# Five of twelve mixer gate pairs as seven block products, in a decoder block on one core

## The chip, the cores and the metric

The kernel runs on one core of a Trainium2 chip. The core has five engines with an instruction stream each: TensorE (PE in the profile, its weight loads PEld), VectorE (DVE), ScalarE (ACT), GpSimd (POOL) and SyncE (SP), which here only starts transfers. Transfers by the core's 16 DMA engines are started from a queue of SP, ACT or POOL. The metric is the device time of one execution in microseconds (us), lower is better; the time before is the median of three runs, 1539.44 us (1537.3 to 1540.5).

## The reference

One decoder block, fp32, 256 tokens, D = 2048. Cut to what matters:

```python
proj = rmsnorm(x, mix_norm_w) @ w_in        # q, k, v, g, gk_low, gate_b, gate_c, xc, merge_a, merge_b
o    = rmsnorm(gla_chunked(q, k, v, log_g), gla_norm_w)          # 4 heads of 512 values
y_a  = o * silu(g)
y_b  = gate_b * causal_depthwise_conv(gate_c * xc, conv_w)       # 3 taps over tokens
merged = sigmoid(merge_a) * y_a + sigmoid(merge_b) * y_b
h    = x + merged @ w_out
gate, up = split(rmsnorm(h, ffn_norm_w) @ w_gate_up)             # 2 x 5632 columns
h    = h + (silu(gate) * up) @ w_down
out  = rmsnorm(h, final_norm_w)
```

The six gates g, gate_b, gate_c, xc, merge_a and merge_b have 2048 columns each. They are the names g, gb, gc, xc, ma and mb below, each cut into four groups of 512 columns (gc0 to gc3 and so on), and fg, fu are the halves of w_gate_up.

## The kernel before

**Precision and tiling.** Every fp32 operand is held as two parts, hi (rounded, made by a cast on ScalarE, L200) and lo (the remainder, a subtraction on VectorE, L205). A product takes three matmuls (lo by hi, hi by lo, hi by hi, L309 to L311 in `mm3`). The two token halves of 128 (t = 0, 1) are the stationary side, and 512 weight columns move, so a group of 512 columns costs 16 row chunks x 2 token halves x 3 = 96 matmuls of 128x512. Weights come in pieces of 128x1024 (512 KB, two row chunks of 512 columns), one DMA each on SP's queue. `stream_list` fixes the order of all pieces, and `load_piece` works five pieces ahead of the one in use: fetch, cast, subtraction. So VectorE's stream is a chain of L205 rows with everything else between them, and it serves TensorE in the order of the pieces. A sum of weights is a piece too: it has its own cast and its own subtraction.

**Stages.** Up to about 206 us: k, q, v of the four heads with the gated linear attention; to 733 us: the 24 gate groups in the order gc, xc, gb, g, ma, mb for each of the four column groups i, all with eight block products; to 824 us: wo (w_out, four groups); then the feed-forward part (FFN) in three parts, each with its hidden groups and then its rows of w_down (dn). Helper work is put into the stream by `later(n, ...)`, `at(n, ...)` and `one_at_a_time(n, ...)`, which run a function when a count of used pieces (the tick) has gone on by n; a scheduler then places each instruction on its engine.

**Block products.** Seen as a product of 2x2 blocks (two token halves by two row chunks on one side, two row chunks by two column groups on the other), a pair of groups needs eight block products, or seven if sums of blocks are multiplied. The FFN before does five of its eleven pairs fg/fu (`SEVEN`, L73) with seven, in `sevens`: 28 pieces of 6 matmuls, 168, where two groups take 192. For each quarter q of the rows the pieces are 11, t1, t3, t2 and t4, and after all quarters 21 and 22; t1 to t4 are sums of weight blocks made by VectorE (L221, L227), and some weight pieces are read twice. The sums of the activations' blocks (hsum, L431 and following) are made when h is transposed. Such a pair is mixed piece by piece with a pair done with eight (`merged`).

**Attention and gates.** In a head, the scores go to PSUM (sc_ps), VectorE masks them (L619) and splits them into sch (ScalarE) and scl (VectorE, L624), and TensorE multiplies them with v (o_ps, `attend`). TensorE takes its instructions in order, so what stands behind an o_ps matmul waits with it. The convolution multiplies u = gc xc and two copies of u shifted by one and two tokens with the taps; the copies are DMAs inside the core's memory, issued on ScalarE's queue (L681 to L686), and VectorE reads them at L692 and L691. A group of merged columns is transposed on TensorE (trb, L440) before wo.

Of the kernel before, what the change touches and what calls it, by code (L numbers as in the profile page):

```python
# [72 lines left out]
SEVEN = (0, 2, 4, 6, 9)  # L73
# [12 lines left out]
def seven_list(f):  # L86

    out = [(what, q) for q in range(4) for what in ("11", "t1", "t3", "t2", "t4")]
    return [(f"s{f}", e) for e in out + [(what, q) for q in range(4) for what in ("21", "22")]]


def eight_list(f):
    return [(f"{m}{f}", k) for m in ("fg", "fu") for k in range(0, KC, 2)]


SPREAD = (("t1", "t3", "t2", "t4"), ("21", "22"))


def merged(part):

    f0, f1 = PARTS[part]
    sevens = [e for f in range(f0, f1) if f in SEVEN for e in seven_list(f)]
    eights = [e for f in range(f0, f1) if f not in SEVEN for e in eight_list(f)]

    gaps = [0] * len(sevens)
    rest = len(eights)
    while rest > 0:
        for some in SPREAD:  # L110
            for n, e in enumerate(sevens):
                if e[1][0] in some and rest > 0:
                    gaps[n] += 1
                    rest -= 1
# [4 lines left out]
    return out + eights[put:]  # L119


def down_list(part):

    f0, f1 = PARTS[part]
    ends = {}
    for i, (key, _) in enumerate(merged(part)):
        ends[int(key.lstrip("sfgu"))] = i
# [10 lines left out]
def stream_list():  # L138

    pieces = [(p[0], p[3]) for p in piece_list()]  # L140
    out = [e for e in pieces if e[0][:2] not in ("fg", "fu", "dn")]
    for part in range(len(PARTS)):
        out += merged(part)
        out += down_list(part)
# [4 lines left out]
def block_kernel(ctx, tc, x, xt, cols_in, gkw_in, gku_in, gnw, conv_w, finw, w_in, w_out, w_gu, w_dn, out):  # L149
# [4 lines left out]
    res = ctx.enter_context(tc.tile_pool(name="res", bufs=1))  # L154
# [4 lines left out]
    aT = ctx.enter_context(tc.tile_pool(name="aT", bufs=1))  # L159
    psum = ctx.enter_context(tc.tile_pool(name="psum", bufs=1, space=bass.MemoryType.PSUM))  # L160
# [46 lines left out]
    def sum_of(key, what, q):  # L207

        fg, fu = key.replace("s", "fg"), key.replace("s", "fu")
        if what == "21":  # L210
            return fetch(fg, 4 * q + 2)
        if what == "22":
            return fetch(fu, 4 * q + 2)
        if what == "11":
            held["y"] = fetch(fg, 4 * q, dpool, "y")
            return held["y"]
        y = held["y"]
        if what == "t1":
            held["x"] = fetch(fu, 4 * q, dpool, "x")
# [3 lines left out]
        if halfway and halfway[-1][0] is held["x"]:  # L223
            finish_low()
        other = y if what == "t2" else fetch(fu if what == "t3" else fg, 4 * q + 2)
        x = held["x"]
# [86 lines left out]
    def tok_piece(ps, t, piece, k0, first, last, ah, al):  # L313
# [684 lines left out]
```

## Time and profile before

| what | value |
|---|---|
| runs before, median (lowest to highest) | 1539.44 us (1537.3 to 1540.5) |
| profiled execution: its own time, its span | 1539.7 us, 1537.7 us |
| clock granted to TensorE in it | 0.998 |
| busy: TensorE, VectorE, ScalarE | 99%, 68%, 50% of the span |
| matmuls (profiled), pieces of weights | 7249, 612 |

A row of a timeline reads: start in us, duration in us, engine, line of the kernel, operation, output<-inputs, shape, xcount, and in brackets how long the engine sat idle before it and what released it. Successive rows of VectorE overlap by some hundredths of a us, so the time from start to start is the price of a row in a full stream. The table of windows gives for each stretch its length, then the busy time of PE, PEld, DVE, ACT and POOL with their counts, the granted clock, the share of the DMA engines and GB/s.

### The profile page before, as it was taken

The numbers are of one execution on the slowest core, as the hardware profiler recorded it, in microseconds if no ns is written. First come the engines' busy times: TensorE is split into PE (matmuls) and PEld (weight loads), VectorE is DVE, ScalarE is ACT, GpSimd is POOL, SyncE is SP. The second block draws the span as 40 slices with busy tenths as digits, with TensorE's granted clock in tenths as the row PEclk, the third lists the DMA queues.
The fourth block names the chain that finished last, engine by engine and source line by source line (L and its number), as shares of the span: only waits on it lengthen the run. The fifth ranks groups of instructions, "written<-read, shape, count | busy, mean of one in ns | idle before, by whom it ended". The sixth has DMA issues, their size and how long they took to land.

```text
span 1537.7 us, 19268 instructions
## 1 busy us (share of the span) xinstructions
PE 1526.0 (99%) x7249; PEld 1279.2 (83%) x7249; DVE 1040.8 (68%) x1047; ACT 771.8 (50%) x870; POOL 17.7 (1%) x29
## 2 busy tenths in 40 slices
PE   9999999999999999999999999999999999999998
PEld 8989988888888888888888888788888888888887
DVE  6765545655655655465668999855899985678764
ACT  6763454444344344444556565643555653455543
POOL 0020000000000000000000000000000000000000
PEclk9999999999999999999999999999999999999999
DMA  9655566766866666666755877866677886566772
GB/s 321 220 165 177 175 197 190 244 194 192 239 193 191 211 221 190 203 208 194 230 174 176 259 225 236 302 212 181 219 247 222 266 273 195 180 221 202 248 222 92
DMA packets 91846, 327.11 MB, mean 213 GB/s; under 512 B 10381, under 2 KB 10509, under 8 KB 91625
## 3 DMA queue, kind: packets, MB, share of 16 engines
q1 hardware_dynamic: 88320, 316.99, 65.3%
q10 hardware_dynamic: 3432, 8.89, 2.4%
q8 instruction: 57, 0.93, 0.3%
q14 instruction: 37, 0.30, 0.1%
HBM read 319.57 MB, written 2.10 MB: 209 GB/s over the span
## 4 chain that ended last, share of the span: by engine, by line
PE 92%; DVE 4%; issue 1%; DMA 1%; ACT 1%; POOL 1%; DVEq 0%; SPq 0%; ACTq 0%
PE dn L309 5%; PE dn L311 5%; PE dn L310 5%; PE p L309 3%; PE p L311 3%; PE p L310 3%; PE fu L309 3%; PE fu L310 3%; PE fu L311 3%; PE fg L310 2%; PE fg L311 2%; PE fg L309 2%; PE wo L310 2%; PE gc L311 2%; PE mb L310 2%; PE ma L310 2%
## 5 line engine op out<-in xcount | busy, mean ns | idle before, releaser
L205 DVE TENSOR_TENSOR lo<-raw,hi 128x1024 fp32r<-128x1024 f32 (+1 forms) x533 | 648.6, 1221 | 369.0 <-PE dn L309 73.0
L200 ACT CAST hi<-raw 128x1024 fp32r<-128x1024 f32 (+1 forms) x533 | 556.8, 1051 | 566.8 <-PE dn L311 113.9
L309 PE MATMUL dn<-lo,acth 128*128 128x512 f32 (+1 forms) x376 | 141.9, 377 | 0.2 <-DVE sg L810 0.2
L310 PE MATMUL dn<-hi,actl 128*128 128x512 f32 (+1 forms) x376 | 141.2, 376 | 0.0
L311 PE MATMUL dn<-hi,acth 128*128 128x512 f32 (+1 forms) x376 | 141.1, 376 | 0.0
L200 ACT CAST hi<-x 128x1024 fp32r<-128x1024 f32 x60 | 63.2, 1054 | 104.0 <-DVE x L227 68.0
L205 DVE TENSOR_TENSOR lo<-x,hi 128x1024 fp32r<-128x1024 f32 x60 | 73.4, 1223 | 19.9 <-ACT hi L200 12.5
L309 PEld LDWEIGHTS dn<-lo,acth 128*128 128x128 f32 x376 | 70.8, 188 | 13.6 <-DVE sg L810 0.6
L311 PEld LDWEIGHTS dn<-hi,acth 128*128 128x128 f32 x376 | 70.8, 188 | 12.8
L310 PEld LDWEIGHTS dn<-hi,actl 128*128 128x128 f32 x376 | 70.8, 188 | 12.7
L309 PE MATMUL fu<-lo,hh 128*128 128x512 f32 x192 | 74.9, 390 | 0.2 <-DVE sg L810 0.2
L311 PE MATMUL fg<-hi,hh 128*128 128x512 f32 x192 | 74.9, 390 | 0.0
L309 PE MATMUL fg<-lo,hh 128*128 128x512 f32 x192 | 74.8, 390 | 0.0
L310 PE MATMUL fg<-hi,hl 128*128 128x512 f32 x192 | 74.8, 390 | 0.0
L310 PE MATMUL fu<-hi,hl 128*128 128x512 f32 x192 | 74.7, 389 | 0.0
L311 PE MATMUL fu<-hi,hh 128*128 128x512 f32 x192 | 74.7, 389 | 0.0
L309 PE MATMUL p<-lo,sh 128*128 128x512 f32 x160 | 62.9, 393 | 0.0
L311 PE MATMUL p<-hi,sh 128*128 128x512 f32 x160 | 62.4, 390 | 0.0
L310 PE MATMUL p<-hi,sl 128*128 128x512 f32 x160 | 62.3, 390 | 0.0
L227 DVE TENSOR_TENSOR x<-x,raw 128x1024 f32<-128x1024 f32 x40 | 48.8, 1220 | 2.5 <-DMA raw<-in_w_gu_dram 2.3
L309 PE MATMUL v<-lo,xh 128*128 128x512 f32 x128 | 50.4, 394 | 0.0
L309 PE MATMUL wo<-lo,mh 128*128 128x512 f32 x128 | 50.2, 392 | 0.0
(236 smaller groups left out, 3152.5 us busy)
## 6 DMA issues: line engine op xcount, KB each, us to landing
raw<-in_w_in_dram SPq DMA_DIRECT2D x255, 512.0 KB, 4.3
raw<-in_w_gu_dram SPq DMA_DIRECT2D x176, 512.0 KB, 4.6
raw<-in_w_dn_dram SPq DMA_DIRECT2D x88, 512.0 KB, 4.4
raw<-in_w_out_dram SPq DMA_DIRECT2D x32, 512.0 KB, 3.6
y<-in_w_gu_dram SPq DMA_DIRECT2D x20, 512.0 KB, 3.7
x<-in_w_gu_dram SPq DMA_DIRECT2D x20, 512.0 KB, 5.5
u<-u ACTq DMA_DIRECT2D x8, 448.0 KB, 7.2
taps<-in_conv_w_dram ACTq DMA_DIRECT2D x4, 768.0 KB
```

The costliest lines, as they stand in the source:

```text
L200: nc.scalar.copy(hi[:, ks, :], raw[:, ks, :])
L205: nc.vector.tensor_tensor(out=lo[:, ks, :], in0=raw[:, ks, :], in1=hi[:, ks, :].bitcast(F32), op=ALU.subtract)
L227: nc.vector.tensor_tensor(out=x, in0=x, in1=other, op=ALU.add)
L309: nc.tensor.matmul(ps, lhsT=sh, rhs=ml, start=first, stop=False, skip_group_check=onto)
L310: nc.tensor.matmul(ps, lhsT=sl, rhs=mh, start=False, stop=False, skip_group_check=onto)
L311: nc.tensor.matmul(ps, lhsT=sh, rhs=mh, start=False, stop=last, skip_group_check=onto)
```

## The change

**Gates.** Five pairs, (gc0,xc0), (gc1,xc1), (gc2,xc2), (gc3,xc3) and (gb3,mb3), are done as seven block products. `GATES` gives six steps; in each the 28 pieces of the pair are mixed with the pieces of the eight-product groups beside it, in step 4 with a gap after the 11 pieces too. Steps 1 to 5 hold 2, 3, 4, 2 and 2 eight-product groups. The sums of blocks of x that the pairs need (`x_blocks`, four quarters of L714, four L438 and one L440 on VectorE, one cast on ScalarE) are made during attention. `HIDDEN` writes down the same mix for the FFN as before. The pieces grow from 612 to 672, the matmuls fall by 120.

**Element-wise work.** SiLU comes from ScalarE in one activation instead of a sigmoid and a multiplication on VectorE, for g and in the FFN. The head outputs o are normed in `head_norm` during attention, one head at a time, instead of in the gates. gb0 to gb2 leave PSUM by ScalarE. The sigmoids of ma0 to ma3 and mb0 to mb2 go to one buffer, scr, from which VectorE multiplies (L848). The convolution is cut into `conv_shift` (the copies) and `conv_sum` (VectorE's five rows L827 to L831). ScalarE now changes between SiLU and sigmoid in the gates: it has 17 table loads instead of 10.

**Buffers and transfers.** h is no tile of its own during the mixer any more. x is read for its squares into two buffers taken in turn (xq), and again, late, into h: four transfers of 512 KB from GpSimd's queue behind wo's first group.

```diff
-SEVEN = (0, 2, 4, 6, 9)
+GATES = (
+    (None, ("g0",)),
+    (("gc0", "xc0"), ("ma0", "gb0")),
+    (("gc1", "xc1"), ("mb0", "g1", "ma1")),
+    (("gc2", "xc2"), ("gb1", "mb1", "g2", "ma2")),
+    (("gc3", "xc3"), ("gb2", "mb2")),
+    (("gb3", "mb3"), ("g3", "ma3")),
+)
...
+HIDDEN = (
+    ((("fg0", "fu0"), ("fg1", "fu1")), (("fg2", "fu2"), ("fg3", "fu3"))),
+    ((("fg4", "fu4"), ("fg5", "fu5")), (("fg6", "fu6"), ("fg7", "fu7"))),
+    ((("fg9", "fu9"), ("fg8", "fu8", "fg10", "fu10")),),
+)
...
+def mixed(step, early=False):
+
+    pair, keys = step
...
+        for some in (sums + ("11",) if early else sums, ("21", "22")):
+            for n, (_, e) in enumerate(sevens):
...
+def gates_list():
+    return [e for i, step in enumerate(GATES) for e in mixed(step, i == 4)]
...
+    def eights(key, a, done, tags=("b5", "ax1")):
...
+    def sevens(name, pool, a, s, second, done):
...
+            elif what == "t2":
+                quad(pc, lambda j: s(1, q, j), piece, first, last)
+                if last:
+                    u[1] = second(1)
+                    nc.vector.tensor_tensor(out=v2, in0=pc, in1=v2, op=ALU.subtract)
+                    nc.vector.tensor_tensor(out=v3, in0=pd, in1=v2, op=ALU.add)
+                    nc.vector.tensor_tensor(out=u[1], in0=pb, in1=v3, op=ALU.add)
+            elif what == "t4":
+                quad(pe, lambda j: a(1, 4 * q + 2 + j), piece, first, last)
+                if last:
+                    nc.vector.tensor_tensor(out=v3, in0=pe, in1=v3, op=ALU.subtract)
+                    done(1, v3, u[1])
...
+    def sum_blocks(raw, q, tiles, work):
+
+        hi, lo = tiles
+        a11, a21 = raw[:, 0:2, 0:P], raw[:, 0:2, P:T]
+        a12, a22 = raw[:, 2:4, 0:P], raw[:, 2:4, P:T]
+        for s, p, m in ((0, a21, a22), (1, a11, work[:, 0]), (2, a21, a11), (3, a12, work[:, 1])):
+            nc.vector.tensor_tensor(out=work[:, s], in0=p, in1=m, op=ALU.subtract)
+        nc.scalar.copy(hi[:, q], work)
+        nc.vector.tensor_tensor(out=lo[:, q], in0=work, in1=hi[:, q].bitcast(F32), op=ALU.subtract)
...
+    xq = {}
+
+    def load_x(j):
+        xq[j] = gpool.tile([P, NT, 512], F32, tag=("exk", "exq")[j % 2], name="xq")
+        nc.sync.dma_start(xq[j], xv[:, :, j * 512:(j + 1) * 512])
...
+    def x_blocks(q):
+        pair = gpool.tile([P, NM, T], F32, tag="bc", name="xraw")
+        raw, work = pair[:, 0:4, :], pair[:, 4:8, :].rearrange("p s (j c) -> p s j c", c=P)
+        cs = slice(4 * q, 4 * q + 4)
+        nc.vector.tensor_tensor(out=raw, in0=xh[:, cs, :].bitcast(F32), in1=xl[:, cs, :].bitcast(F32), op=ALU.add)
+        sum_blocks(raw, q, xsums, work)
+
+    for q in range(4):
+        at(34 + 6 * q, lambda q=q: x_blocks(q))
...
+    def head_norm(i):
+        rstd_of(sso[:, :, i], DV, ro[:, :, i])
+        for t in range(NT):
+            nc.vector.scalar_tensor_tensor(out=o[i][:, t, :], in0=o[i][:, t, :], scalar=ro[:, t, i:i + 1], in1=gnb,
+                                           op0=ALU.mult, op1=ALU.mult)
...
+    def gated(dst, ps):
+
+        for t in range(NT):
+            scr = ew.tile([P, 512], F32, tag="scr", name="scr")
+            nc.scalar.activation(scr, ps[t], AF.Sigmoid, scale=r1[:, t:t + 1])
+            nc.vector.tensor_tensor(out=dst[:, t, :], in0=dst[:, t, :], in1=scr, op=ALU.mult)
...
+    def gate(key):
+        i = int(key[-1])
+
+        def done(ps):
+            if key[:-1] == "g":
+                ya[i] = ew.tile([P, NT, 512], F32, tag="ya", name="ya")
+                for t in range(NT):
+                    nc.scalar.activation(ya[i][:, t, :], ps[t], AF.Silu, scale=r1[:, t:t + 1])
+                nc.vector.tensor_tensor(out=ya[i], in0=ya[i], in1=o[i], op=ALU.mult)
+            elif key[:-1] == "gb":
+                sb[i] = ew.tile([P, NT, 512], F32, tag="sb", name="sb")
+                for t in range(NT):
+                    nc.scalar.activation(sb[i][:, t, :], ps[t], AF.Copy, scale=r1[:, t:t + 1])
+            elif key[:-1] == "ma":
+                gated(ya[i], ps)
+            else:
+                gated(sb[i], ps)
+                merge(i, slice(0, NT))
...
+            if pair[0][:-1] == "gc":
+                nc.vector.scalar_tensor_tensor(out=two, in0=one, scalar=r1sq[:, t:t + 1], in1=two,
+                                               op0=ALU.mult, op1=ALU.mult)
+                if t == 0:
+                    later(2, lambda: conv_shift(i))
+                    later(8, lambda: conv_sum(i))
+            else:
+                nc.scalar.activation(two, two, AF.Sigmoid, scale=r1[:, t:t + 1])
+                nc.vector.scalar_tensor_tensor(out=two, in0=one, scalar=r1[:, t:t + 1], in1=two,
+                                               op0=ALU.mult, op1=ALU.mult)
+
+                later(3 if t else 1, lambda: merge(i, slice(t, t + 1)))
...
+    steps = run(gates_list(), begin_gate)
+    for n in steps:
...
+        if h is None:
+            mix.close()
+            dpool = ctx.enter_context(tc.tile_pool(name="dpool", bufs=1))
+            h = dpool.tile([P, NT, D], F32, name="h")
+            for j in range(4):
+                nc.gpsimd.dma_start(h[:, :, j * 512:(j + 1) * 512], xv[:, :, j * 512:(j + 1) * 512])
...
-        nc.scalar.activation(dst, src, AF.Sigmoid, scale=r2[:, t:t + 1])
-        times(dst, src, t)
+        nc.scalar.activation(dst, src, AF.Silu, scale=r2[:, t:t + 1])
```

VectorE in attention, where the scores of heads 0 and 1 are masked and split (L741 and L746 after are L619 and L624 before). Before:

```order
L603 TENSOR_TENSOR exk<-exk,kr 128x256
L205 TENSOR_TENSOR lo<-raw,hi 128x1024 x3
L619 COPY_PREDICATED scr<-mask,sc_ps 128x256
L624 TENSOR_TENSOR scl<-scr,sch 128x384
L205 TENSOR_TENSOR lo<-raw,hi 128x1024
L619 COPY_PREDICATED scr<-mask,sc_ps 128x256
```

And with the change, from the row behind exk on, where L714, L438 and L440 are `x_blocks`:

```order
L714 TENSOR_TENSOR xraw<-xh,xl 128x1024
L222 TENSOR_TENSOR lo<-raw,hi 128x1024
L438 TENSOR_TENSOR xraw<-xraw 128x256 x3
L222 TENSOR_TENSOR lo<-raw,hi 128x1024
L438 TENSOR_TENSOR xraw<-xraw 128x256
L222 TENSOR_TENSOR lo<-raw,hi 128x1024
L440 TENSOR_TENSOR sl<-xraw,sh 128x1024
L741 COPY_PREDICATED scr<-mask,sc_ps 128x256
L714 TENSOR_TENSOR xraw<-xh,xl 128x1024
L746 TENSOR_TENSOR scl<-scr,sch 128x384
L222 TENSOR_TENSOR lo<-raw,hi 128x1024
L438 TENSOR_TENSOR xraw<-xraw 128x256 x2
```

The second mask (L741) is the next row. Six instructions of sums stand ahead of the first mask and three more between it and the second; TensorE's order there is as before.

VectorE where the third convolution begins, before (xc, the third group of its kind) and with the change (start of step 4):

```order
L205 TENSOR_TENSOR lo<-raw,hi 128x1024 x13
L711 SCALAR_TENSOR_TENSOR u<-xc_0_4123,r_117,u 128x512
L205 TENSOR_TENSOR lo<-raw,hi 128x1024
L711 SCALAR_TENSOR_TENSOR u<-xc_1_4124,r_117,u 128x512
L694 TENSOR_TENSOR yb<-u,taps 128x1024
L205 TENSOR_TENSOR lo<-raw,hi 128x1024
L692 TENSOR_TENSOR u_4294<-u_4294,taps 128x1024
```

```order
L411 TENSOR_TENSOR u<-gc_1_3847,v_3851 128x512
L882 SCALAR_TENSOR_TENSOR u<-gc_0_3846,r1sq,u 128x512
L222 TENSOR_TENSOR lo<-x,hi 128x1024
L848 TENSOR_TENSOR ya<-ya,scr 128x512
L244 TENSOR_TENSOR x<-x,y 128x1024
L848 TENSOR_TENSOR ya<-ya,scr 128x512
L828 TENSOR_TENSOR u_4836<-u_4836,taps 128x1024
L222 TENSOR_TENSOR lo<-raw,hi 128x1024
```

Between the last write of u and the first row that reads a copy (L692, now L828) lay two rows of VectorE, and now lie four; the rows around it now belong to a stream with sums of weights in it (L244).

ScalarE at the same place with the change, where L814 to L819 issue the copies:

```order
L847 ACT_TABLE_LOAD
L847 ACTIVATE scr<-ma_0_4595,r_115 128x512
L814 DMA u_4836<-u 112x1024
L847 ACTIVATE scr<-ma_1_4596,r_115 128x512
L815 DMA u_4836<-u 15x1024
```

A table load and the sigmoid of ma2 stand ahead of the first copy; before, the copies stood ahead of or between casts only.

More of the change, by code (lines that the diff above doesn't have):

```diff
@@ L109, in merged @@
     while rest > 0:
-        for some in SPREAD:
-            for n, e in enumerate(sevens):
-                if e[1][0] in some and rest > 0:
+        for some in (sums + ("11",) if early else sums, ("21", "22")):
+            for n, (_, e) in enumerate(sevens):
+                if e[0] in some and rest > 0:
                     gaps[n] += 1
```

424 lines of the change are left out of this document (205 added, 219 removed).

## The prediction

> **What bounds the kernel now.** I read the page first: its head, its first part and the chain of the work that ended last.
>
> ```profile
> span 1537.7 us, 19268 instructions
> PE 1526.0 (99%) x7249; PEld 1279.2 (83%) x7249; DVE 1040.8 (68%) x1047; ACT 771.8 (50%) x870; POOL 17.7 (1%) x29
> PE 92%; DVE 4%; issue 1%; DMA 1%; ACT 1%; POOL 1%; DVEq 0%; SPq 0%; ACTq 0%
> ```
>
> TensorE is busy nearly throughout and is the chain, so a matmul taken away is time, if VectorE (68% on average) can still feed it. That average hides two kinds of stages, which the table of windows parts. Its rows are attention around head 0, the 24 gate groups, and the first two FFN hidden parts:
>
> ```profile
> core 0: us, PE busy (x) PEld busy (x) DVE busy (x) ACT busy (x) POOL busy (x), PEclk, DMA share, GB/s
> 82.00:108.00 26.00, 25.05 (x122) 20.55 (x121) 16.72 (x25) 17.12 (x21) 5.67 (x7) 1.00 0.57 181
> 206.00:733.00 527.00, 527.00 (x2338) 436.75 (x2337) 299.02 (x274) 230.34 (x239) 4.08 (x8) 1.00 0.68 206
> 823.70:992.40 168.70, 168.38 (x758) 138.13 (x756) 157.73 (x155) 103.52 (x116) 0.00 (x0) 1.00 0.77 248
> 1080.60:1247.60 167.00, 166.88 (x749) 137.62 (x748) 154.03 (x147) 96.39 (x102) 0.00 (x0) 1.00 0.76 250
> ```
>
> In the gates VectorE works 299 of 527 us, 57%; in the hidden parts, where half the pairs are done as sevens already, 158 of 168.7, 93%. The groups of VectorE in the gates say what it does in its idle time there:
>
> ```profile
> L205 DVE TENSOR_TENSOR lo<-raw,hi 128x1024 fp32r<-128x1024 f32 x192 | 234.5, 1224 | 192.8 <-PE xc L309 42.7 <-PE mb L309 37.3 <-PE ma L309 35.9
> ```
>
> Its 192.8 us of idling before L205 ended with TensorE: it waits for buffers, so it is ahead. The change spends this spare time to buy matmuls.
>
> **The saving.** One matmul's price is the distance of starts in the gates, here the first and the 57th row of TensorE's timeline:
>
> ```profile
> 379.65 0.39 PE L309 MATMUL xc<-lo,xh 128*128 128x512 f32 x1
> 392.35 0.39 PE L311 MATMUL gb<-hi,xh 128*128 128x512 f32 x1
> ```
>
> 12.70 us / 56 = 0.2268 us. A pair falls from 192 to 168 matmuls; five pairs save 120 x 0.2268 = 27.2 us. All else is what VectorE loses of it.
>
> **VectorE in the gates.** Its prices come from a full stretch of the FFN, start to start:
>
> ```profile
> 922.37 1.22 DVE L205 TENSOR_TENSOR lo<-y,hi 128x1024 fp32r<-128x1024 f32 x1
> 923.50 1.22 DVE L205 TENSOR_TENSOR lo<-raw,hi 128x1024 fp32r<-128x1024 f32 x1
> 924.64 1.22 DVE L227 TENSOR_TENSOR x<-x,raw 128x1024 f32<-128x1024 f32 x1
> 925.78 1.22 DVE L205 TENSOR_TENSOR lo<-raw,hi 128x1024 fp32r<-128x1024 f32 x1
> ...
> 929.34 1.22 DVE L227 TENSOR_TENSOR x<-x,y 128x1024 f32<-128x1024 f32 x1
> 931.75 1.23 DVE L205 TENSOR_TENSOR lo<-x,hi 128x1024 fp32r<-128x1024 f32 x1 [1.20 <-ACT hi L200]
> ```
>
> A row of 128x1024 costs 1.136 us ((925.78 - 922.37) / 3). Where a sum of weights and its own subtraction are neighbours, VectorE also waits for the cast between them, 1.20 us. A product row of 128x512 costs about 0.66, a sum 0.60, read from these:
>
> ```profile
> 96.88 0.68 DVE L603 TENSOR_TENSOR ek<-ek,kr 128x512 f32<-128x512 f32 x1
> 97.48 0.42 DVE L603 TENSOR_TENSOR exq<-exq,qr 128x256 f32<-128x256 f32 x1
> ...
> L810 DVE SCALAR_TENSOR_TENSOR sg<-fg,r,sg 128x512 f32<-128x512 f32 x12 | 8.7, 746 | 1.5 <-ACT sg L806 1.5
> ```
>
> (97.48 - 96.88 = 0.60; 0.746 less the overlap of 0.085 between 1.22 and 1.136.) A seven pair with one eight pair now takes 28 + 16 = 44 subtractions and 16 sums, 60 large rows; the FFN pair of steps is that, and with 9 sums and 8 products comes to 60 x 1.136 + 9 x 0.60 + 8 x 0.66 = 78.9 us, against 360 matmuls x 0.2268 = 81.6. It fits: two such steps are 163.3 us of matmuls, and the windows above are 168.7 and 167.0, 4 to 5 us more for eight transposed blocks and all waits.
>
> By the changed order's rows (its large rows, sums, products) the gate steps are: step 1, 62, 6, 1: 74.7 against 81.6; step 2, 76, 9, 2: 93.1 against 103.4; step 3, 84, 11, 2: 103.4 against 125.2; step 4, 67, 11, 2: 84.0 against 81.6; step 5, 65, 10, 2: 81.2 against 81.6. The convolution's five large rows and the masks of the gates do this: steps 4 and 5 have no room. They also hold 4 and 5 neighbours of sum and subtraction in the order: 4.8 and 6.0 us at 1.20 each.
>
> Then there are the copies of u. Before, VectorE waited for them, at little cost:
>
> ```profile
> 252.53 0.75 DVE L711 SCALAR_TENSOR_TENSOR u<-xc,r,u 128x512 f32<-128x512 f32 x1
> 253.31 0.57 ACTq L681 DMA_DIRECT2D u<-u  x1
> 261.55 1.23 DVE L692 TENSOR_TENSOR u<-u,taps 128x1024 f32<-128x1024 f32 x1 [5.87 <-DMA u<-u]
> ...
> 515.48 0.75 DVE L711 SCALAR_TENSOR_TENSOR u<-xc,r,u 128x512 f32<-128x512 f32 x1
> 516.25 0.56 ACTq L681 DMA_DIRECT2D u<-u  x1
> 522.16 1.23 DVE L692 TENSOR_TENSOR u<-u,taps 128x1024 f32<-128x1024 f32 x1 [3.54 <-DMA u<-u]
> ```
>
> A copy is usable 5.9 (522.16 - 516.25) to 8.2 us (261.55 - 253.31) after its issue. In step 4 the new order has L222, L848, L244, L848 between u and L828, 2 x 1.136 + 2 x 0.60 = 3.5 us, and the issue waits behind a table load and a sigmoid on ScalarE (order of ScalarE), about 1.3 us more: 5.9 + 1.3 - 3.5 = 3.7 to 8.2 + 1.3 - 3.5 = 6.0. I take 5. In step 5's conv 5.7 us of work lie between: 0.2 to 2.5, I take 1. Behind L828 stand all subtractions of the next pieces, and TensorE waits for those once its five pieces of lead are gone.
>
> Steps 4 and 5 together: 84.0 + 81.2 + 4.8 + 6.0 + 5 + 1 = 182.0 us of VectorE. TensorE has 163.2 of matmuls and, four transposed blocks, 1.8 at 0.46 each (an upper bound: the 3.7 us above over eight blocks). The lead of five pieces takes 5 x 1.136 = 5.7. Loss 182.0 - 165.0 - 5.7 = 11.3. In steps 2 and 3 the average has room (10 and 22 us), but each has a lump, copies and merge rows ahead of a transpose; I take 2 each. Gates: **+15**, between 6 (the 4 of steps 2 and 3, and 2 where copies land in time and neighbours hide) and 31 (rival D).
>
> The table loads in this rest on one row:
>
> ```profile
> 59.74 1.07 ACT L200 CAST hi<-raw 128x1024 fp32r<-128x1024 f32 x1
> 60.83 1.28 ACT L590 ACT_TABLE_LOAD   x1
> 62.12 1.92 ACT L590 ACTIVATE za<-za 128x2048 f32<-128x2048 f32 x1
> ```
>
> Seven more loads are 9 us of ScalarE, which works 230 of 527 us in the gates: hidden, except the one ahead of the copy, counted above. The Trainium skill (ScalarE: Activation LUTs, section What ACT_TABLE_LOAD costs) speaks against the change more strongly: about 1283 ns for the load and a drain of about 1380 ns beside it. Here the load is 1.28 us and starts 0.02 us after the cast ends, with no drain to be seen; the rule would make the copy of step 4 some 1.4 us later and the sum 1.4 us higher. I go by the row.
>
> **Attention.** The sums of x cost VectorE 4 x (2 x 1.136 + 4 x 0.336), 14.5 us, and they stand in the score chain:
>
> ```profile
> 97.82 0.41 DVE L603 TENSOR_TENSOR exk<-exk,kr 128x256 f32<-128x256 f32 x1
> 98.16 3.49 DVE L205 TENSOR_TENSOR lo<-raw,hi 128x1024 fp32r<-128x1024 f32 x3
> 101.56 0.44 DVE L619 COPY_PREDICATED scr<-mask,sc_ps 128x256 f32<-128x256 int8 x1
> 102.88 0.56 DVE L624 TENSOR_TENSOR scl<-scr,sch 128x384 fp32r<-128x384 f32 x1 [0.88 <-ACT sch L622]
> 103.36 1.22 DVE L205 TENSOR_TENSOR lo<-raw,hi 128x1024 fp32r<-128x1024 f32 x1
> 104.49 0.43 DVE L619 COPY_PREDICATED scr<-mask,sc_ps 128x256 f32<-128x256 int8 x1
> 105.33 0.50 PE L309 MATMUL o_ps<-vl,sch 128*128 128x512 f32 x1 [0.95 <-ACT scr L620]
> ```
>
> (0.336 is 97.82 to 98.16 for 128x256.) Ahead of the first mask come 2 x 1.136 + 4 x 0.336 = 3.6 us more, ahead of the second 1.136 + 2 x 0.336 more, of which 0.88 fill the wait for sch: 0.9. TensorE already waits for this chain in the last row, so it gets there 4.5 us later, and what follows for the next head I put at 1.5: **+6**, between 0 (the scheduler's rows run in TensorE's slack after all) and 6. head_norm's work moves from the gates to here, 8 rows of 0.66, beside TensorE's matmuls for the next head.
>
> **The rest.** SiLU takes about 22 products off the FFN, 14.5 us of VectorE, some 2.6 per pair of steps; since VectorE there ends just inside TensorE's time, only waits go: -1, between -3 and 0. A SiLU by ScalarE has no row; it lies between the casts and sigmoids of the same shape, and ScalarE is busy 104 of 168.7 us. x for the squares: SP's load waits for a buffer; behind it are weight pieces that are already some transfers ahead; 0, up to 2. h late: the transfers start about 11 us into wo0 and are wanted at its end, 21.8 us (96 x 0.2268); 512 KB pieces land in 4 us or so:
>
> ```profile
> raw<-in_w_out_dram SPq DMA_DIRECT2D x32, 512.0 KB, 3.6
> ```
>
> 0, up to 3, since GpSimd's own transfers of this size have no row.
>
> **Sum** against the profiled execution's 1539.7 us (its span 1537.7 and 2.0 around it; the median of the runs is 0.3 lower): 1539.7 - 27.2 + 15 + 6 - 1 = 1532.5, rounded with the median to **1532**.
>
> **Rivals.** B, VectorE keeps the FFN's pace in the gates: the copies land before they are read and neighbours are hidden. Gates cost 6: 1523.5. For it: steps 4 and 5 hold as many rows as FFN steps, which lose little. Against: L692 waited for the copies (row under D). C, attention hides its sums too and the gates lose nothing beyond 1: about 1511.5, the whole saving and SiLU's -1. Against: the chain of masks is tight in the rows above. D, slower: the copies. They share the DMA engines with eight more weight pieces per pair. If landing grows with the engines' share (0.77 in the FFN's window, 0.68 in the gates'), 8.2 becomes 9.3 and the wait 9.3 + 1.3 - 3.5 = 7.1. With four copies at 6.5, between that and the 6.0 above, the gates lose 11.3 - 6 + 26 = 31, and the time is 1548.5. It decides from a loss of 22 in the gates, (22 - 5.3) / 4 = 4.2 us a copy. For it: such waits were there in all four before, hidden by VectorE's slack:
>
> ```profile
> DVE u L692 <- DMA u<-u: 17.1, 4, 5.9
> ```
>
> Against: steps 2 and 3 have 10 and 22 us of room for it.
>
> E, the clock. The window 82 to 108 had 0.95 us of idle TensorE and a clock of 1.00. If a stall of 4.5 us drops the clock for a few us, about 3.5 us more: 1535.5. The Trainium skill (TensorE: Matmul & The Clock Gate, section Part 1: The HAM clock gate) has such a rule: an idle window of about 3.4 us halves the clock. No row here has so long a stall inside the stream.
>
> **How the numbers follow.** Chances: forecast 0.47, B 0.22, C 0.08, D 0.18, E 0.05. The forecast's own range is 1527 to 1538. The range for 8 in 10 leaves out C and half of D: 1516 to 1546. A measurement tells 0.2%, 3.1 us, from no change: faster is below 1536.4, slower above 1542.5. Faster: B, C, most of the forecast (0.36) and a little of E, 0.68; slower: most of D, 0.17; the same 0.15.
>
> **What would show it.** TensorE's matmuls should fall by 120 and its timeline keep 0.2268 us between starts. Right: idle time on TensorE ahead of o_ps of heads 0 and 1 (4 to 5 us, released by VectorE or sch), and ahead of matmuls of steps 4 and 5, released by lo (L222), with VectorE above 95% there; L828 waiting on u's copies in step 4. Wrong: TensorE idle less than 8 us in the gates (B), no wait at o_ps (C), L828 waiting 6 us or more in each convolution (D), or a clock below 1 near 105 us (E). The FFN's windows should shrink by at most 3 us in all; if they shrink more, I undervalued SiLU.

## The result, and the profile after

The changed kernel takes 1553.64 us (median of four runs, 1552.18 to 1556.43) against 1539.12 for the kernel before: ratio 1.0097, 95% interval 1.0079 to 1.0116. It is 14.5 us slower, where 1532 was forecast, some 7 us faster than before. The page's head, busy line and chain of waits of the changed kernel (this execution took 1552.18 us):

```profile
span 1550.3 us, 19386 instructions
PE 1508.5 (97%) x7129; PEld 1256.5 (81%) x7129; DVE 1205.4 (78%) x1208; ACT 839.4 (54%) x947; POOL 20.8 (1%) x33
PE 85%; DVE 5%; DMA 4%; issue 2%; ACT 2%; POOL 1%; ACTq 0%; SPq 0%; DVEq 0%
```

The 120 matmuls are gone (7249 to 7129). But TensorE fell from 92% to 85% of the chain, and DMA rose from 1% to 4%, ScalarE from 1% to 2%: things that hardly anything waited for before are on the path now.

The windows of the changed kernel, cut at its own stages (attention around heads 0 and 1, the gates, wo, the first two FFN hidden parts; columns as before):

```profile
82.00:114.00 32.00, 27.60 (x120) 21.77 (x119) 24.75 (x38) 19.50 (x24) 5.71 (x7) 0.90 0.51 153
212.50:745.00 532.50, 508.50 (x2222) 413.85 (x2220) 453.83 (x421) 289.02 (x307) 4.08 (x8) 0.99 0.75 242
745.00:836.80 91.80, 90.55 (x412) 74.99 (x413) 64.44 (x68) 51.69 (x67) 3.02 (x4) 1.00 0.67 219
836.80:1005.50 168.70, 168.25 (x758) 138.38 (x757) 155.20 (x150) 105.10 (x117) 0.00 (x0) 1.00 0.75 251
1093.60:1260.20 166.60, 166.60 (x750) 137.92 (x749) 152.17 (x142) 98.70 (x104) 0.00 (x0) 1.00 0.77 254
```

Against the windows of before: the gates begin 6.5 us later (206.0, now 212.5) and last 5.5 us longer (527.0, now 532.5) instead of 27.2 shorter; wo is 1.1 longer; from the first FFN matmul to the end it is 713.5 us (1550.3 - 836.8) against 714.0. So attention lost 6.5 us, as forecast, and the gates lost 27.2 + 5.5 = 32.7, where 15 were forecast.

**Attention.** TensorE's timeline of the changed kernel at the first o_ps, and a window behind it:

```profile
106.60 0.49 PE L326 MATMUL o_ps<-vl,sch 128*128 128x512 f32 x1 [2.86 <-ACT sch L744]
107.35 0.79 PE L327 MATMUL o_ps<-vh,scl 128*128 128x512 f32 x1 [0.25 <-DVE scl L746]
...
109.86 0.79 PE L326 MATMUL o_ps<-vl,sch 128*128 128x512 f32 x1 [1.29 <-ACT scr L742]
110.45 0.63 PE L327 MATMUL o_ps<-vh,scl 128*128 128x512 f32 x1
110.87 0.63 PE L328 MATMUL o_ps<-vh,sch 128*128 128x512 f32 x1
```

```profile
110.00:114.00 4.00, 4.00 (x10) 3.13 (x11) 3.81 (x5) 3.94 (x8) 0.31 (x1) 0.50 0.44 142
```

The stalls sum to 4.4 us (0.95 before). Behind them the granted clock is 0.50, and matmuls start 0.42 us apart (110.45 to 110.87) instead of 0.227. So 3.5 of the 6.5 us are the longer stall, and the other 3 are left for the clock.

**Gates.** Their longest stall lies in step 2, where the first convolution begins. ScalarE, VectorE and TensorE of the changed kernel there:

```profile
322.20 0.63 ACTq L814 DMA_DIRECT2D u<-u  x1
322.86 1.37 ACTq L815 DMA_DIRECT2D u<-u  x1
...
326.37 1.30 ACTq L819 DMA_DIRECT2D u<-u  x1
327.77 1.05 ACT L217 CAST hi<-raw 128x1024 fp32r<-128x1024 f32 x1 [5.10 <-DVE raw L238]
```

```profile
325.63 1.23 DVE L238 TENSOR_TENSOR raw<-y,x 128x1024 f32<-128x1024 f32 x1
330.63 1.23 DVE L828 TENSOR_TENSOR u<-u,taps 128x1024 f32<-128x1024 f32 x1 [3.77 <-DMA u<-u]
333.36 1.23 DVE L244 TENSOR_TENSOR x<-x,raw 128x1024 f32<-128x1024 f32 x1 [1.50 <-DMA raw<-in_w_in_dram]
```

```profile
329.74 0.39 PE L328 MATMUL gc<-hi,sh 128*128 128x512 f32 x1
335.77 0.79 PE L326 MATMUL mb<-lo,xh 128*128 128x512 f32 x1 [5.65 <-DVE lo L222]
```

Three things happen at once. ScalarE issues six copies from 322.2 to 327.7 us and casts nothing. VectorE's L828 waits 3.77 us for a copy. And a weight piece comes late; the chain of waits of the changed kernel gives its transfer 7.54 us, where the page's median for pieces of w_in is 4.5:

```profile
325.73 7.54 DMA raw<-in_w_in_dram
...
334.50 1.23 DVE lo L222
```

Without the copies the piece fetched at this place (325.66 us in no_copy, below) landed after 4.5 us. Two of the three, the issues and a copy, stand in the chain in step 5 too, one behind the other:

```profile
655.50 0.59 ACTq L814
656.12 2.76 ACTq L815
659.00 1.06 ACT hi L217
660.11 1.11 issue
661.22 1.22 DVE lo L222
662.43 1.15 DVE x L244
663.97 4.97 DMA u<-u
```

What VectorE waited for in the gates (212.5 to 745 us) of the changed kernel, as sum, times and longest:

```profile
DVE lo L222 <- ACT hi L217: 37.5, 37, 2.7
DVE u L828 <- DMA u<-u: 15.3, 4, 5.0
```

The four waits for copies are 3.77, 4.99, 4.60 and 1.93 us, at the convolutions in steps 2 to 5. The windows of these four steps say where the time went. First the changed kernel, then no_copy, the experiment below that leaves the copies out (one profile each); a stretch starts with the first matmul of the step's pair:

```profile
319.10:431.00 111.90, 106.25 (x465) 87.47 (x464) 96.91 (x91) 59.29 (x63) 1.03 (x2) 0.97 0.78 250
431.00:560.60 129.60, 126.93 (x562) 104.22 (x561) 106.09 (x98) 69.86 (x74) 1.03 (x2) 1.00 0.75 241
560.60:652.50 91.90, 84.80 (x369) 67.60 (x367) 78.87 (x74) 45.32 (x50) 1.03 (x2) 1.00 0.72 227
652.50:745.00 92.50, 84.55 (x366) 67.43 (x364) 82.73 (x79) 51.67 (x55) 0.00 (x0) 1.00 0.76 247
```

```profile
319.10:424.90 105.80, 105.23 (x465) 85.97 (x464) 96.43 (x91) 59.33 (x63) 1.03 (x2) 1.00 0.78 254
424.90:554.00 129.10, 126.59 (x561) 104.22 (x560) 106.50 (x98) 70.72 (x74) 1.04 (x2) 1.00 0.72 234
554.00:640.40 86.40, 84.43 (x369) 69.30 (x369) 79.57 (x74) 47.06 (x51) 1.03 (x2) 0.98 0.72 235
640.40:729.70 89.30, 84.28 (x366) 67.59 (x365) 84.94 (x79) 51.85 (x55) 0.00 (x0) 1.00 0.76 248
```

| step | matmuls at 0.2268, us | the change, us | no_copy, us | copies (difference), us |
|---|---|---|---|---|
| 2 | 103.4 | 111.9 | 105.8 | 6.1 |
| 3 | 125.2 | 129.6 | 129.1 | 0.5 |
| 4 | 81.6 | 91.9 | 86.4 | 5.5 |
| 5 | 81.6 | 92.5 | 89.3 | 3.2 |

In steps 4 and 5 of the changed kernel VectorE is busy 86% and 89% of the time, not above 95% as forecast: it waits there.

So two theories stood against each other. W: the copies carry the surplus (first as the wait at their reader). N: VectorE simply has too many rows in steps 4 and 5.

### The profile page after: what moved, and what is told of

It reads as the page before. It is cut to its first block, busy times and chain, and to the rows that moved or that the text cites. A ratio compares the mean times of both kernels' runs of the same rounds, so it can differ in the third digit from the quotient of the medians.

```text
span 1550.3 us, 19386 instructions
## 1 busy us (share of the span) xinstructions
PE 1508.5 (97%) x7129; PEld 1256.5 (81%) x7129; DVE 1205.4 (78%) x1208; ACT 839.4 (54%) x947; POOL 20.8 (1%) x33
## 4 chain that ended last, share of the span: by engine, by line
PE 85%; DVE 5%; DMA 4%; issue 2%; ACT 2%; POOL 1%; ACTq 0%; SPq 0%; DVEq 0%
PE fg L326 7%; PE fg L328 7%; PE fg L327 7%; PE dn L326 5%; PE dn L328 5%; PE dn L327 5%; DVE lo L222 3%; PE fu L326 3%; PE fu L327 3%; PE fu L328 3%; PE gc L326 2%; PE gc L328 2%; PE gc L327 2%; DMA raw<-in_w_in_dram 2%; PE ma L326 2%
## 5 line engine op out<-in xcount | busy, mean ns | idle before, releaser
L217 ACT CAST hi<-x 128x1024 fp32r<-128x1024 f32 x120 | 126.3, 1053 | 230.6 <-DVE x L244 153.4
L222 DVE TENSOR_TENSOR lo<-x,hi 128x1024 fp32r<-128x1024 f32 x120 | 146.8, 1223 | 45.4 <-ACT hi L217 32.3
L326 PE MATMUL fg<-lo,hh 128*128 128x512 f32 x312 | 122.6, 393 | 0.0
L327 PE MATMUL fg<-hi,hl 128*128 128x512 f32 x312 | 121.6, 390 | 0.0
L244 DVE TENSOR_TENSOR x<-x,raw 128x1024 f32<-128x1024 f32 x80 | 97.6, 1220 | 4.9 <-DMA raw<-in_w_in_dram 2.6
L328 PEld LDWEIGHTS fg<-hi,hh 128*128 128x128 f32 x312 | 58.6, 188 | 12.4
L326 PEld LDWEIGHTS fg<-lo,hh 128*128 128x128 f32 x312 | 58.6, 188 | 12.3 <-ACT hraw L534 0.3
L327 PEld LDWEIGHTS fg<-hi,hl 128*128 128x128 f32 x312 | 58.6, 188 | 11.7
L326 PE MATMUL fg<-lo,sh 128*128 128x512 f32 x160 | 62.9, 393 | 0.0
L328 PE MATMUL fg<-hi,sh 128*128 128x512 f32 x160 | 62.4, 390 | 0.0
```

Of the source, the lines that this page charges most:

```text
L217: nc.scalar.copy(hi[:, ks, :], raw[:, ks, :])
L222: nc.vector.tensor_tensor(out=lo[:, ks, :], in0=raw[:, ks, :], in1=hi[:, ks, :].bitcast(F32), op=ALU.subtract)
L244: nc.vector.tensor_tensor(out=x, in0=x, in1=other, op=ALU.add)
L326: nc.tensor.matmul(ps, lhsT=sh, rhs=ml, start=first, stop=False, skip_group_check=onto)
L327: nc.tensor.matmul(ps, lhsT=sl, rhs=mh, start=False, stop=False, skip_group_check=onto)
L328: nc.tensor.matmul(ps, lhsT=sh, rhs=mh, start=False, stop=last, skip_group_check=onto)
```

## The experiments

All are edits of the changed kernel. The gates' length is from the gates' first matmul (g0; gc0 in the kernel before) to the first of wo in one profile each (532.5 in the changed kernel, 527.0 before); times are medians. The runs of one kernel spread by 1.2 to 9.2 us (pool_copy the most, 1534.46 to 1543.67), so a difference of 1 or 2 us between two medians shows little. In each kernel the scheduler orders the instructions anew, so the price of an edit holds its new order too. no_copy and tiny_copy leave out a part of the computation.

| kernel | time, us | ratio to before (95% interval) | gates, us |
|---|---|---|---|
| the change | 1553.64 | 1.0097 (1.0079 to 1.0116) | 532.5 |
| no_pairs | 1539.10 | 0.9999 (0.9990 to 1.0008) | 527.6 |
| x_late | 1550.12 | 1.0071 (1.0056 to 1.0086) | 537.9 |
| conv_late | 1547.28 | 1.0057 (1.0042 to 1.0072) | 529.3 |
| no_copy | 1534.09 | 0.9967 (0.9955 to 0.9980) | 516.9 |
| tiny_copy | 1541.15 | 1.0012 (1.0003 to 1.0021) | 522.4 |
| both_late | 1542.43 | 1.0018 (1.0005 to 1.0031) | 529.9 |
| pool_copy | 1539.92 | 1.0003 (0.9991 to 1.0015) | 523.9 |
| pool_late | 1532.93 | 0.9965 (0.9954 to 0.9976) | 522.9 |
| spread | 1537.24 | 0.9987 (0.9978 to 0.9996) | 526.6 |
| sp_late | 1532.06 | 0.9947 (0.9930 to 0.9963) | 523.9 |
| late_four | 1534.62 | 0.9971 (0.9962 to 0.9981) | 523.9 |
| pool_four | 1530.21 | 0.9943 (0.9927 to 0.9958) | 518.5 |
| pool_even | 1528.97 | 0.9935 (0.9922 to 0.9949) | 518.4 |
| pool_four_even | 1527.73 | 0.9927 (0.9915 to 0.9940) | 517.7 |

### no_pairs: everything but the pairs

```diff
-    (("gc0", "xc0"), ("ma0", "gb0")),
+    (None, ("gc0", "xc0", "ma0", "gb0")),
...
-    for q in range(4):
-        at(34 + 6 * q, lambda q=q: x_blocks(q))
```

> All 24 gate groups with eight block products, in the order of the change's steps, and no sums of x; SiLU on ScalarE, head_norm, the early x, the late h and the split convolution stay. Theory: the rest of the change costs nothing (0 to -2 us), so 1537 to 1540, and the whole loss of 14.5 us comes with the pairs. Rival: the late h, the table loads or head_norm cost something by themselves: 1543 or more, and the pairs are then dearer by that much less.

(Not shown: gc and xc get PSUM buffers and rows of their own again.) Measured 1539.10, ratio 0.9999. The rest of the change (SiLU, head_norm, early x, late h, table loads, the split convolution) is worth nothing in sum, and the whole loss comes with the pairs and their sums. This kernel issues the same 24 copies from ScalarE, and so does the kernel before: where VectorE is ahead, they cost nothing that shows. The window of its gates is nearly the one of before, with TensorE full:

```profile
205.80:733.40 527.60, 527.58 (x2339) 436.24 (x2338) 289.30 (x256) 243.08 (x253) 4.08 (x8) 1.00 0.69 208
```

### x_late: the sums of x out of the score chain

```diff
+        nc.vector.tensor_copy(raw[:, 0, 0:1], o[1][:, 0, 0:1])
         nc.vector.tensor_tensor(out=raw, in0=xh[:, cs, :].bitcast(F32), in1=xl[:, cs, :].bitcast(F32), op=ALU.add)
...
+        if i == 1:
+            for q in range(4):
+                at(tick_of + 2 + 3 * q, lambda q=q: x_blocks(q))
```

> The sums of x are made to follow the output of head 1 (a copy of 128x1 from it into their buffer ahead of each quarter), so that no row of theirs stands ahead of the masks of heads 0 and 1. Theory: they alone made TensorE wait 3.5 us longer at o_ps, and the lower clock behind that stall (0.50 to 0.55 from 107 to 114 us) cost another 3; both vanish, attention ends near 206 instead of 212.5 us, and the time falls by 6.5 to about 1547, with no clock below 1 before 206 us. Rival: the work is merely late elsewhere in attention, where VectorE also feeds TensorE, and the time stays within 2 us of 1553.6. A third reading, that only the clock matters and the stall stays: about 1551.

Measured 1550.12: 3.5 us won, half of the forecast. In attention it went as the theory says: the gates begin at 205.9 us, 6.6 earlier, and the window of this kernel has its clock back:

```profile
82.00:114.00 32.00, 31.02 (x159) 25.70 (x158) 20.84 (x32) 23.41 (x30) 5.31 (x7) 1.00 0.57 178
```

But the gates lasted 537.9 instead of 532.5 us. The waits for copies grew, 18.0 us in the four (longest 6.5) against 15.3. So the attention term stands, and part of its gain went into the loss that the other runs are about.

### conv_late: the readers of the copies later

```diff
+        for tap in (0, 1):
+            nc.vector.scalar_tensor_tensor(out=taps[:, tap, 0:1], in0=held["lo"][:, 0, 0:1].bitcast(F32), scalar=0.0,
+                                           in1=taps[:, tap, 0:1], op0=ALU.mult, op1=ALU.add)
         nc.vector.tensor_tensor(out=u2, in0=u2, in1=taps_of(0), op=ALU.mult)
```

> The two rows of the convolution that read the shifted copies are tied to a later piece (rows of 128x1 write the first column of their taps from a lo piece times zero), so that 9 to 13 rows of VectorE instead of 0 to 4 lie between u and them. Theory W (the waits for the copies of u carry the surplus): VectorE's 15.3 us of waits there vanish, and with them TensorE's 7.6 us in step 2, 1.4 in step 3, some 4 in step 4 and 2 in step 5; the time falls by 13 to 15, to about 1540. Theory N (VectorE has too many rows in steps 4 and 5, whatever it waits for): only steps 2 and 3 win, 7 to 9 us, to about 1546, and the idle time of TensorE from 580 to 690 us stays above 10 us.

Measured 1547.28: 6.4 us won, not 13 to 15. No wait for a copy is left on VectorE at all, but the stall in step 2 is. VectorE's timeline of this kernel at that place:

```profile
325.88 1.23 DVE L238 TENSOR_TENSOR raw<-y,x 128x1024 f32<-128x1024 f32 x1 [0.27 <-DMA y<-in_w_in_dram]
333.35 1.23 DVE L244 TENSOR_TENSOR x<-x,raw 128x1024 f32<-128x1024 f32 x1 [6.24 <-DMA raw<-in_w_in_dram]
```

With the reader out of the way, the same time is spent waiting for a weight piece. The wait at the reader, on which the forecast and the slower rival both rested, had only been the last of several things that came late together. By the number alone theory N fits, though TensorE's idle time from 580 to 690 us, which N has above 10 us, came to 9.4; the next run speaks against it.

### no_copy: no copies at all

```diff
-        nc.scalar.dma_start(u1[1:113, :, :], u[0:112, :, :])
...
-        nc.vector.tensor_tensor(out=u2, in0=u2, in1=taps_of(0), op=ALU.mult)
+        nc.vector.tensor_tensor(out=u2, in0=u, in1=taps_of(0), op=ALU.mult)
```

> Leaves out the shifted copies: the convolution reads u itself for all three taps, with the same VectorE rows and none of the six transfers per group on ScalarE's queue. It gives the price of the copies whole: waits, the 5.5 us in which ScalarE issues them and casts stand behind, and their share of the DMA engines. Theory W: about 1540, as when the rows come later. If issuing them on ScalarE is a cost of its own: 3 us or more below the kernel with the later rows. Theory N: not below 1545.

Measured 1534.09: 19.5 us won, with the same rows on VectorE; 15.6 of them lie in the gates of the two profiled executions (532.5 to 516.9). The copies cost three times what later readers won back. So theory W is wrong in its mechanism: it is not the reader's wait alone. Theory N, as the whole cause, is out too, but the gates without copies still lose 17.1 of the 32.7 us, and that part is not the copies'.

### tiny_copy: the issues without the bytes

```diff
-        nc.scalar.dma_start(u1[1:113, :, :], u[0:112, :, :])
+        nc.scalar.dma_start(u1[1:113, :, 0:8], u[0:112, :, 0:8])
...
```

> The change with the six copies cut to 8 of 512 columns and the convolution reading u itself (a part of the computation left out): the issues on ScalarE's queue stay, the bytes go, and the first row of the convolution still waits for the small copies to land. Theory I: the casts still stand behind the issues, 1545 or more. Theory B: near the kernel without copies, 1534 to 1537, since only the bytes made the weight pieces late.

Measured 1541.15, between the two: six small transfers per convolution cost 7.1 us more than none (the issues, and the 5.2 us that VectorE still waited for them), the bytes and their landing 12.5. Neither theory I nor theory B holds alone.

### both_late, pool_late, pool_copy: who issues

```diff
-        nc.scalar.dma_start(u1[1:113, :, :], u[0:112, :, :])
+        nc.gpsimd.dma_start(u1[1:113, :, :], u[0:112, :, :])
...
```

(all six; both_late has the edits of x_late and conv_late, pool_late those and this one, pool_copy this one alone.)

> The later sums of x and the later reads of the copies together. Apart they gave 3.5 and 6.4 us; the sums moved out of the score chain gave 6.6 in attention, but the gates then waited 5 us more for the copies. If that give-back is the wait at the copies' reader, it cannot come back here: 1553.6 - 6.6 - 6.4 = 1540.6. If it is the copies' load on the DMA engines, the two add as measured, about 1543.7.

> The same with the six copies of each convolution issued by GpSimd instead of ScalarE. Theory I (issuing: ScalarE spends about 5.5 us per group on the six issues, and the casts of the next pieces stand behind them): 6 us or more below the kernel with both later, about 1533. Theory B (bytes: 1 MB of copies ahead of weight pieces on the DMA engines, so that the pieces land late): the same as that kernel within 2 us, and VectorE still waits about 6 us for a weight piece near 326 us.

> The change with one edit: the six copies of each convolution are issued by GpSimd instead of ScalarE; the rows that read them stay where they are. Between the two kernels with later rows this edit gave 9.5 us. If the issues on ScalarE are a cost of their own (the casts behind them): about 1544, 8 to 11 us below the change. If they cost only together with where the rows lie, or if the wait at the copies' reader grows by as much: 1549 or more, with VectorE's wait there above 15.3 us.

Measured 1542.43, 1532.93 and 1539.92. The two later edits roughly add up: 11.2 us together, 3.5 and 6.4 apart. Moving six issues per convolution from ScalarE to GpSimd wins 9.5 us beside them, and 13.7 alone, with the same bytes. VectorE's timelines at the first convolution, first of both_late, then of pool_late:

```profile
318.11 1.23 DVE L238 TENSOR_TENSOR raw<-y,x 128x1024 f32<-128x1024 f32 x1
325.99 1.22 DVE L244 TENSOR_TENSOR x<-x,raw 128x1024 f32<-128x1024 f32 x1 [6.66 <-DMA raw<-in_w_in_dram]
```

```profile
319.03 1.22 DVE L238 TENSOR_TENSOR raw<-y,x 128x1024 f32<-128x1024 f32 x1
320.32 1.22 DVE L222 TENSOR_TENSOR lo<-x,hi 128x1024 fp32r<-128x1024 f32 x1
321.46 1.22 DVE L222 TENSOR_TENSOR lo<-raw,hi 128x1024 fp32r<-128x1024 f32 x1
322.60 1.22 DVE L222 TENSOR_TENSOR lo<-y,hi 128x1024 fp32r<-128x1024 f32 x1
323.73 1.22 DVE L222 TENSOR_TENSOR lo<-raw,hi 128x1024 fp32r<-128x1024 f32 x1
326.20 1.23 DVE L835 TENSOR_TENSOR u<-u,taps 128x1024 f32<-128x1024 f32 x1 [1.25 <-DMA u<-u]
```

The weight piece is late in both: fetched at 318.16 us it is read at 325.99 in both_late, and in pool_late the piece fetched at 318.01 landed after 7.7 us. So here who issues did not change what the bytes do to the piece. But in pool_late casts go on during the copies, and four subtractions are there to be done while the piece that L244 needs is under way. In both_late the casts stand behind the issues, and VectorE's order has L244 ahead of those subtractions; it stops there until the piece lands, although the casts that they need end between 320.94 and 323.78 us. TensorE then stalls 5.84 us, in pool_late 1.35 in two parts. So the edit is not pure: it moves ScalarE's work and with it VectorE's order, and at this place the order is what holds VectorE. In pool_copy, too, the readers moved back by themselves, and VectorE's waits for copies fell from 15.3 to 3.0 us.

### spread, sp_late: the block of issues or the queue

```diff
+        def copy(n, to, of):
+            later(n, lambda: nc.scalar.dma_start(to, of))
+
-        nc.scalar.dma_start(u2[2:114, :, :], u[0:112, :, :])
+        copy(3, u2[2:114, :, :], u[0:112, :, :])
...
```

(spread, on both_late, has its reads one piece later as well, `later(9, ...)` for `later(8, ...)`; sp_late is pool_late with `nc.sync` in place of `nc.gpsimd`.)

> Later sums of x and later reads, copies from ScalarE, but the six issues of a convolution are put one to three pieces apart, so that casts stand between them; bytes, queue and readers stay. Issuing them from GpSimd gave 9.5 us against the block of six (1542.4 to 1532.9). If the block of issues ahead of the casts was the cost: near 1533, at most 1536, and TensorE's stall of 5.8 us in step 2 shrinks to about 2. If ScalarE's queue itself is the cost (its transfers take the DMA engines from the weight pieces in another way than GpSimd's): 1540 or more.

> The same with the six issues from SP's queue, on which the weight pieces are fetched: no cast stands behind them, but a fetch does while SP waits for u. If only the casts matter: 1533 to 1536. If a transfer that waits on SP holds back the pieces behind it: slower than with ScalarE's block, 1543 or more.

Measured 1537.24 and 1532.06, the first between its two forecasts. Casts between the issues win 5.2 us of the 9.5 on the same queue, though this edit also spreads the bytes in time; taking the issues off ScalarE wins the rest, and SP does as well as GpSimd although it fetches the weights too. So it matters that the block of issues stands in ScalarE's order; the likeliest reason is ScalarE's time, which each issue takes from casts, but that ScalarE's queue has a part in the last 4 us is not excluded. What part goes through VectorE's changed order, and what directly through late casts, these runs don't part. The sum of VectorE's waits for casts does not follow the time: 37.7 us in the gates of sp_late, 37.5 in those of the change, which is 21.6 us slower.

### late_four, pool_four, pool_even, pool_four_even: which pairs pay

```diff
-    (("gb3", "mb3"), ("g3", "ma3")),
+    (None, ("gb3", "g3", "ma3", "mb3")),
...
-    (("gc2", "xc2"), ("gb1", "mb1", "g2", "ma2")),
-    (("gc3", "xc3"), ("gb2", "mb2")),
+    (("gc2", "xc2"), ("gb1", "mb1", "g2")),
+    (("gc3", "xc3"), ("ma2", "gb2", "mb2")),
```

(the first is "four", on both_late or pool_late; the second "even". With four pairs, g3 and mb3 get other PSUM buffers.)

> Both later, and the fifth pair (gb3, mb3) done with eight block products, so that four pairs remain. The pair saves 24 matmuls, 5.4 us; the change lost about 10 us of TensorE time between 630 and 690 us, where it stands. If VectorE's rows of that step cause the loss: 4 us or more below the kernel with both later. If the loss there comes from step 4's end (merge, transposes and the last block sums of gc3), it stays and the kernel is 3 to 5 us slower than that one.

> Later sums of x, later reads, copies from GpSimd, and the fifth pair with eight block products. Two estimates: from the five-pair kernel with all three (1532.9), the pair's 5.4 us come back and TensorE's 7.7 us of loss between 640 and 670 go, 1530; from the four-pair kernel with copies on ScalarE (1534.6), its 8.4 us of stall in step 2 go, 1526. Theory: the fifth pair does not pay even with cheap copies, so below 1532.9. Rival: with the issues off ScalarE the fifth pair pays, 1534 or more.

> Five pairs, the three edits, and ma2 moved from step 3 to step 4, so that both hold three eight-product groups. By rows, step 4 then has about 108 us of matmuls against 84 + 26 us ... of which the moved group brings its own eight subtractions: VectorE 84 + 8 x 1.136 + 1.2 = 94.3 against 81.6 + 21.8 = 103.4 for TensorE; step 3 falls to 93 against 103.4. Theory N: the 5 us of loss at the end of step 4 (620 to 640 us) vanish and step 3 takes on no more than 1: about 1528 to 1529. If that loss comes from the order at the border (merge ahead of the last block sums, transposes waiting) and not from the number of rows, it stays: 1532 to 1534.

> Four pairs, the three edits and the moved ma2. If both estimates hold, 1526 to 1530 less 4 to 5: 1522 to 1526, the fastest kernel here; four pairs alone save 21.8 us of matmuls, so the floor is about 1517.5 + 1. If the border of steps 4 and 5 keeps its loss, as for the four-pair kernel without it.

Measured 1534.62, 1530.21, 1528.97 and 1527.73. Beside copies on ScalarE the fifth pair cost 7.8 us net (1542.43 to 1534.62), although it saves 5.4 of matmuls; with copies on GpSimd 2.7 (1532.93 to 1530.21). Moving ma2 to step 4 won 4.0 us with five pairs, as expected by the rows, and 2.5 with four, less than expected. Here theory N has a part: steps 4 and 5 have too little TensorE time for VectorE's rows and its waits between them. pool_four_even has the lowest median, 11.4 us (0.73%) below the kernel before; its 1.2 us to pool_even are within the spread. Its page:

```profile
span 1527.0 us, 19399 instructions
PE 1508.7 (99%) x7153; PEld 1261.5 (83%) x7153; DVE 1173.5 (77%) x1185; ACT 831.3 (54%) x936; POOL 33.2 (2%) x57
```

TensorE is back at 99%.

## Why the prediction was wrong

**The saving** of 27.2 us was right: 120 matmuls, 0.2268 us each. The FFN at -1 was right too (-0.5 here; -1.5 in no_pairs, whose time is that of before), as were the zeros for the early x and the table loads; wo took 1.1 us more than before, but not for the late h: no_pairs has it too, and its wo took 90.8 us, 0.1 more than before. Two small slips in the sums changed nothing: the pair of steps in the FFN adds up to 78.8 us, and the two windows there are 5.4 and 3.7 us above 163.3.

**Attention, +6**, was right as a sum (6.5) and half wrong in its making, so the number is partly luck. I had 4.5 us of stall and 1.5 for what follows; it was 3.5 of stall and 3 that are left for the clock, which rival E had at 0.05. x_late gave it back (6.6 us in attention), so the sums of x ahead of the masks are its cause.

**The step that failed is the gates' +15, in its term for the copies**: "In step 4 ... I take 5. In step 5's conv ... I take 1." It priced the copies as a wait at their first reader in two of four steps, 6 us, and left steps 2 and 3 at 2 us each for all their lumps, because "the average has room". Where it priced the wait, the wait came as forecast: 4.60 and 1.93 us. But by no_copy the copies cost 15.6 us of the gates, 6.6 of them in steps 2 and 3 and 8.7 in steps 4 and 5, and 19.5 us of the whole time. In step 2 an average with 10 us of room did not help: there the copies made a stall of 5.65 us. Not in the sum at all were ScalarE's six issues per convolution, 5.5 us in the first in which no cast is made (7.1 us by tiny_copy with the small copies' landing, 9.5 by pool_late with VectorE's new order), and the weight pieces that land late while 1 MB of copies is under way (7.5 to 7.7 us for those shown, the median 4.5). I had looked at ScalarE's share of busy time, 230 of 527 us, and called its extra work hidden. But issues are not in that share.

**The lead** is the second term that failed. For steps 4 and 5 I had 182.0 us of VectorE: 165.2 of rows, 10.8 of waits for casts and 6 for copies. In the changed kernel, from 560.6 to 745 us, it was 161.6, 14.8 and 6.5, together 182.9, so that sum was right. TensorE needed 165.0, and the two steps took 184.4, so they lost 19.4 us; the forecast of 11.3 had taken off 5.7 for the lead of five pieces, and nothing of that shows. Why the lead did not help was not tried. Without copies, too, the two steps took 175.7 us, 10.7 above 165.0.

**VectorE's rows** were the smaller error. Without copies the gates still lost 527.0 - 27.2 - 516.9, that is 17.1 us, where the forecast without its copy term is 9; of these 8 us 5.4 lie in steps 4 and 5, where the lead had been taken off. That steps 4 and 5 have no room was right: the two edits that relieve these steps won 4.0 (pool_even) and 2.7 us (pool_four). Which rows make up the rest was not tried.

**The rivals.** D, slower by the copies, named the place, and its number came near (a loss of 31 in the gates, 32.7 measured; 1548.5 with attention's 6), but by luck: it had 26 us for copies, 6.5 at each reader, and 5.3 for the rest, where no_copy has 15.6 and 17.1, and the readers waited 3.8 us on average. B and C are out. E came true beside the forecast, not in its place.

## What to carry to other kernels

An average of 57% on a helper engine is not spare time for a new scheme: count, step by step, what stands in its order ahead of the bounding engine's next need, and count for each queue owner the time it spends issuing, which its busy share does not show. Count the steps with room as well: 10 us of room on average did not keep a stall out of step 2. When a wait is cured and the time hardly moves, look at what was late behind it: here a copy, a cast and a weight piece were late together, and only leaving out the copies whole, then their bytes alone, gave prices. Issue transfers from an engine whose next work nobody waits for, here GpSimd; SP, which fetches the weights, did as well.

## What the runs showed of the hardware

The granted clock fell behind stalls of TensorE. In the changed kernel, after stalls of 4.4 us in 6 (attention) and 5.65 us (step 2) it was 0.50 to 0.58, and matmuls took 0.42 us; after stalls of 2.43 us and less it stayed at 1.00. But the length of a stall alone does not decide: in x_late a stall of 1.95 us was followed by a clock of 0.57, in pool_late one of 2.81 us by 1.00. The windows behind the stalls, the changed kernel at step 2, x_late, then pool_late:

```profile
336.00:340.00 4.00, 4.00 (x11) 3.15 (x12) 4.00 (x4) 0.00 (x0) 0.00 (x0) 0.58 0.89 308
```

```profile
436.00:440.00 4.00, 3.98 (x11) 3.17 (x12) 4.00 (x4) 0.00 (x0) 0.00 (x0) 0.57 0.69 200
```

```profile
657.30:661.00 3.70, 3.70 (x16) 3.07 (x17) 3.70 (x4) 0.00 (x0) 0.00 (x0) 1.00 0.40 108
```

The Trainium skill (TensorE: Matmul & The Clock Gate, section Part 1: The HAM clock gate) has an idle window of about 3.4 us after which the clock halves. The stall of 5.65 us agrees with it; the one of 1.95 us is shorter than that window and halved the clock all the same, and the measurement decides. The low stretch lasted some 4 us behind the stall of step 2 and some 7 in attention.

In the first convolution six transfers issued by GpSimd took its queue 3.3 us (0.51 to 0.69 each, pool_copy), by ScalarE 5.5 (0.56 to 1.37, the changed kernel, where the longest of all is 2.76). While 1 MB of copies was under way, a weight piece of 512 KB took 7.7 us to land (pool_late), at the same place without copies 4.5 (no_copy). The ACT_TABLE_LOADs, seven more, cost nothing that the runs show: no_pairs has all 17, TensorE is busy 527.58 of 527.60 us of its gates, and its time stands at 0.9999.
